# A hybrid attention layer's adaLN columns: wide products folded by VectorE, or one-column products

## The chip, the cores and the metric

The kernel runs on one core of one Trainium2 chip. The time is the device's time of one execution in microseconds (us); lower is better. A core has TensorE (PE, matrix products, with a weight load ahead of each product, PEld), VectorE (DVE), ScalarE (ACT), GpSimd (POOL) and SyncE (SP, which here only issues DMA transfers). Each engine works through its own queue in order; semaphores tie the queues together.

## The reference

One decoder layer over x of 2048 rows and 1024 columns, float32. Only the beginning matters here:

```python
mod = jax.nn.silu(c) @ w_ada[l] + b_ada[l]
shift, scale, gate = jnp.split(mod, 3, axis=-1)
h = rms_norm(x, g_pre[l]) * (1.0 + scale[:, None, :]) + shift[:, None, :]
proj = h @ w_in[l]
qa, ka, va, fa, za, qb, kb, vb, zb = jnp.split(proj, split_points, axis=-1)
...
y = jnp.concatenate([oa, ob], axis=-1) @ w_out[l]
x = x + gate[:, None, :] * rms_norm(y, g_post[l])
```

c is one row of 1024 numbers and w_ada has 1024 rows and 3 x 1024 columns, so shift and scale are two products of one row with a 1024 x 1024 matrix each. Between the projection and the output lie a causal attention with forget gates (8 heads) and a sliding-window attention with sinks (8 heads); the change doesn't touch them.

## The kernel before

The kernel is one long program. It begins with a block in which it makes the scale and the shift, normalises and turns the first 512 rows of x, and prepares the weights of the first two projections (named kb and vb). Behind the block a list of projection units runs over four chunks of 512 rows (chunk number ci); the next chunk is turned between the units of the present one. Then come window attention, the causal attention and the output projection. The order on each engine around the change is that of the statements, by hand.

**Tiles.** P is 128, KT is 8: the 1024 columns are 8 groups of 128, and k counts them. The projections need x turned: columns on partitions, rows along the tile. `hT[ci]` holds the turned chunk in two float16 parts, a high one and a low one (the rest), so that three float16 products stand for one of more precision.

**Scale and shift** (`half` 1 is the scale, 0 the shift). `load_ada` (L440) brings a part of w_ada, 128 rows by 1024 columns, 512 KB, into one of eight slots `wa`; sixteen parts are loaded, the scale's first. `sil` holds silu(c) as 8 columns; `silb` (L467) is each of these columns repeated 128 times. Each part goes one of two ways. `ada_pe` (L478) multiplies on TensorE with `silb` as weight and the part's columns moving, two products of 512 columns, into two banks of PSUM; so every partition holds the same row of 1024 results. `ada_dve` (L481) multiplies and adds on VectorE into `acc`; `ada_sum` (L488) adds this to the banks by a product with ones. `ada_col` (L491) turns the row into columns: VectorE multiplies each bank with the identity and sums over 128, two instructions a bank, four a half, so that entry (p, k) is result 128 k + p.

**Order of the scale's and shift's work.** On TensorE: six parts of the scale, its sum (L567), a small transpose for the weights' maxima (L572), the shift's parts 0, 3 and 5, later its part 7 and its sum (L603, L604). VectorE has the scale's parts 2 and 5 and the shift's 1, 2, 4 and 6. Four tiles of x (128 rows each, `load_x`) come between the shift's loads 2 and 3, four more behind the last. ScalarE squares each tile of x and sums by row (`squares`, L374); `root` makes the reciprocal root on VectorE, in small instructions; `normal(0)` multiplies the first four tiles by it on ScalarE.

**From the shift to the first turned column.** With the scale come `gcol`, which is g (1 + scale), and its absolute value `absg` (L596, L598); with the shift `shf` (L612) and its absolute value. `bnd` = 32 |gcol| + |shf| bounds what turned x can hold; its maximum over the 8 columns (L618), a transpose (L620), a maximum (L622) and a product with ones (L623) bring the largest one to every partition, and a power of two below it (`pow2_floor`, `pH`) scales `Gp` and `Shp` (L627, L628), which ScalarE's passes use as scale and bias.

**Turned x.** `turn(ci, k)` transposes four blocks on TensorE into one of five PSUM banks of the pool `ps_x` and gives back two steps: `scaled` writes `hf` (float32) and, for even k, the high part, each by a pass of ScalarE (L403); `split` copies the high part on VectorE for odd k (L407) and subtracts it for the low part (L408). In the block five turns stand ahead of the bound's work, then ScalarE squares the second chunk's four tiles (`squares(1)`, L608), and a loop over k (L632) runs the steps, the second chunk's root in parts from k = 2, and the last three turns. Outside the block `turn_x` does the same for the later chunks.

Of the kernel before, what the change touches and what calls it, by code (L numbers as in the profile page):

```python
# [10 lines left out]
F32 = mybir.dt.float32  # L11
# [4 lines left out]
ALU = mybir.AluOpType  # L16
AX = mybir.AxisListType

P = 128
S = 2048  # L20
D = 1024
KT = D // P
NB = S // P
CH = 512
# [17 lines left out]
def hybrid_layer(  # L42
# [17 lines left out]
    V, A, G, PE, SP = nc.vector, nc.scalar, nc.gpsimd, nc.tensor, nc.sync  # L60
# [10 lines left out]
    ps_x = psx.enter_context(tc.tile_pool(name="ps_x", bufs=5, space=PSUM, reuse_waits="tile"))  # L71
# [9 lines left out]
    def sm(n, tag):  # L81
        return small.tile([P, n], F32, tag=tag, name=tag)

    def pow2_floor(dst, src, bits_tag):

        t = sm(1, bits_tag)
        V.tensor_scalar(t[:], src, 1.0e-30, None, op0=ALU.max)
        V.tensor_scalar(dst.bitcast(I32), t[:].bitcast(I32), 0x7F800000, None, op0=ALU.bitwise_and)

    def rsqrt_mean(dst, ss, n):  # L90

        for _ in rsqrt_parts(dst, ss, n):
            pass
# [52 lines left out]
    ident = const.tile([P, P], F32, name="ident")  # L146
# [8 lines left out]
    ones = const.tile([P, P], F32, name="ones")  # L155
    sil = const.tile([P, KT], F32, name="sil")
# [17 lines left out]
    bk = [ps_bk.tile([P, CH], F32, name=f"bk{n}") for n in range(3)]  # L174
# [80 lines left out]
    def w_low(key, part, parts=2):  # L255
        raw, pw, sw, whl = wq[key]
        ks = slice(KT * part // parts, KT * (part + 1) // parts)
        V.scalar_tensor_tensor(whl[:, 1, ks], raw[:, ks], sw[:], whl[:, 0, ks], op0=ALU.mult, op1=ALU.subtract)
        if part == parts - 1:
            wq[key] = whl  # L260
            pws[key] = pw
# [112 lines left out]
    def squares(ci, us=range(4)):  # L374
        if ci not in rstd:
            rstd[ci] = sm(4, "ss"), sm(4, "rst")
        for u in us:
            junk = hst.tile([P, D], BF16, tag="junk", name="junk", bufs=1)
            A.activation(junk[:], xt[ci * 4 + u], AF.Square, accum_out=rstd[ci][0][:, u:u + 1])

    def root(ci):
        ss, rst = rstd[ci]
        rsqrt_mean(rst, ss[:], 4)

    def normal(ci, us=range(4)):
        for u in us:
            t, r = ci * 4 + u, rstd[ci][1][:, u:u + 1]
            if ci == 0:
                A.activation(xt[t], xt[t], AF.Copy, scale=r)
            else:  # L390
                V.tensor_scalar(xt[t], xt[t], r, None, op0=ALU.mult)

    def turn(ci, k):

        px = ps_x.tile([P, CH], F32, tag="x", name="px")
        for u in range(4):
            PE.transpose(px[:, u * P:(u + 1) * P], xt[ci * 4 + u][:, k * P:(k + 1) * P], ident[:])
        hf = hst.tile([P, CH], F32, tag="hf", name="hf")
        hi, lo = hT[ci][:, 0, k, :], hT[ci][:, 1, k, :]

        def scaled():
            for dst in ([hi] if k % 2 == 0 else []) + [hf[:]]:
                A.activation(dst, px[:], AF.Identity, scale=Gp[:, k:k + 1], bias=Shp[:, k:k + 1])  # L403

        def split():
            if k % 2:
                V.tensor_copy(hi, hf[:])  # L407
            V.tensor_tensor(lo, hf[:], hi, op=ALU.subtract)  # L408

        return scaled, split  # L410

    def turn_x(ci, k):
        scaled, split = turn(ci, k)
        after(1, scaled)
        after(2, split)
# [9 lines left out]
    start = ExitStack()  # L425
    st = start.enter_context(tc.tile_pool(name="start", bufs=1, reuse_waits="tile"))
    wad = start.enter_context(tc.tile_pool(name="wad", bufs=8, reuse_waits="tile"))
    with tc.manual_schedule():
# [9 lines left out]
        wa = {}  # L438
# [19 lines left out]
        cols = st.tile([P, 40], F32, name="cols")  # L458
# [4 lines left out]
        V.tensor_scalar(hc[:], cols[:, 0:8], 0.5, None, op0=ALU.mult)  # L463
        V.scalar_tensor_tensor(sil[:], th[:], 1.0, hc[:], op0=ALU.add, op1=ALU.mult)

        silb = st.tile([P, KT, P], F32, name="silb")
        V.tensor_copy(silb[:], sil[:].unsqueeze(2).broadcast_to([P, KT, P]))  # L467

        pm = {1: [ps_x.tile([P, CH], F32, tag="x", name="pm") for _ in range(2)], 0: [bk[1], bk[2]]}
        acc = [st.tile([P, D], F32, name=f"acc{n}") for n in range(2)]

        def ada_mm(half, lhsT, rows_, begin, end):
            for n in range(2):
                PE.matmul(pm[half][n][:], lhsT, rows_[:, n * CH:(n + 1) * CH], start=begin, stop=end)

        def ada_pe(half, k, begin=False, end=False):  # L478
            ada_mm(half, silb[:, k, :], wa[half, k], begin, end)

        def ada_dve(half, k, first_):  # L481
            if first_:
                V.tensor_scalar(acc[half][:], wa[half, k][:], sil[:, k:k + 1], None, op0=ALU.mult)
            else:
                V.scalar_tensor_tensor(acc[half][:], wa[half, k][:], sil[:, k:k + 1], acc[half][:],
                                       op0=ALU.mult, op1=ALU.add)

        def ada_sum(half, end):  # L488
            ada_mm(half, ones[:], acc[half], False, end)

        def ada_col(half, dst):  # L491

            for n in range(2):
                dg = acc[half][:, n * CH:(n + 1) * CH].rearrange("p (k n) -> p k n", k=4)
                V.tensor_tensor(dg, pm[half][n][:].rearrange("p (k n) -> p k n", k=4),
                                ident[:].unsqueeze(1).broadcast_to([P, 4, P]), op=ALU.mult)
                V.tensor_reduce(dst[:, 4 * n:4 * n + 4], dg, axis=AX.X, op=ALU.add)


        zero = st.tile([P, 2 * P], F32, name="zero")  # L500
# [49 lines left out]
        def col8(name):  # L550
            return st.tile([P, KT], F32, name=name)


        for k in (0, 1, 3, 4, 6, 7):
            ada_pe(1, k, k == 0)
# [8 lines left out]
        for t in range(4, 8):  # L564
            load_x(t)
        w_load("zb0", pieces("zb0"), SP)
        ada_sum(1, True)  # L567

        mx3 = st.tile([P, 2], F32, name="mx3")
        for n, key in enumerate(first[:2]):  # L570
            V.tensor_reduce(mx3[:, n:n + 1], wq[key][0][:], axis=AX.XY, op=ALU.max, apply_absolute_value=True)
        PE.transpose(bk[0][0:2, 0:P], mx3[:], ident[:])  # L572
        ada_pe(0, 0, True)
        ada_dve(0, 1, True)
        ada_dve(0, 2, False)
# [3 lines left out]
        V.tensor_scalar(dg3[:], ident[0:2, 0:2], m3[:], None, op0=ALU.mult)  # L579
        PE.matmul(bk[0][:, P:P + 2], ones[0:2, :], dg3[:], start=True, stop=True)  # L580
        ada_pe(0, 3)
        ada_pe(0, 5)
        squares(0)
        scl0 = col8("scl0")
        ada_col(1, scl0)
        V.tensor_copy(mxs[:, 0:2], bk[0][:, P:P + 2])
        for n, key in enumerate(first[:2]):
            wq[key].append(mxs[:, n:n + 1])
# [2 lines left out]
        w_high("kb")  # L591
        w_high("vb")
        scl1 = col8("scl1")
        V.tensor_tensor(scl1[:], scl0[:], cols[:, 24:32], op=ALU.add)
        gcol = col8("gcol")
        V.scalar_tensor_tensor(gcol[:], scl1[:], 1.0, cols[:, 8:16], op0=ALU.add, op1=ALU.mult)  # L596
        absg = col8("absg")
        V.scalar_tensor_tensor(absg[:], gcol[:], -1.0, gcol[:], op0=ALU.mult, op1=ALU.max)  # L598
        root(0)
        normal(0)  # L600
        ada_dve(0, 4, False)
        ada_dve(0, 6, False)
        ada_pe(0, KT - 1)  # L603
        ada_sum(0, True)  # L604
        w_low("kb", 0, 1)
        w_low("vb", 0, 1)
        turned = [turn(0, k) for k in range(5)]
        squares(1)  # L608
        shf0 = col8("shf0")
        ada_col(0, shf0)  # L610
        shf = col8("shf")
        V.tensor_tensor(shf[:], shf0[:], cols[:, 16:24], op=ALU.add)  # L612
        abss = col8("abss")
        V.scalar_tensor_tensor(abss[:], shf[:], -1.0, shf[:], op0=ALU.mult, op1=ALU.max)
        bnd = col8("bnd")
        V.scalar_tensor_tensor(bnd[:], absg[:], 32.0, abss[:], op0=ALU.mult, op1=ALU.add)
        bmx = st.tile([P, 1], F32, name="bmx")
        V.tensor_reduce(bmx[:], bnd[:], axis=AX.X, op=ALU.max)  # L618

        PE.transpose(bk[0][0:1, 0:P], bmx[:], ident[:])  # L620
        bm = st.tile([1, 1], F32, name="bm")
        V.tensor_reduce(bm[:], bk[0][0:1, 0:P], axis=AX.X, op=ALU.max)  # L622
        PE.matmul(bk[0][:, P:P + 1], ones[0:1, :], bm[:], start=True, stop=True)  # L623
        pow2_floor(pH[:], bk[0][:, P:P + 1], "p2t")
        ipH = st.tile([P, 1], F32, name="ipH")
        V.reciprocal(ipH[:], pH[:])
# [5 lines left out]
        for k in range(KT):  # L632
            turned[k][0]()
            turned[k][1]()
            if k >= 2:
                next(root1, None)
            if k + 5 < KT:
                turned.append(turn(0, k + 5))
# [865 lines left out]
    with tc.manual_schedule():  # L1504
# [25 lines left out]
        for s, stp_ in enumerate(steps):  # L1530
# [20 lines left out]
            half = (len(todo) + 1) // 2  # L1551
# [85 lines left out]
```

## Time and profile before

| | us |
|---|---|
| median of 3 runs | 1205.63 |
| lowest, highest | 1203.94, 1209.42 |
| the profiled execution | 1204.7 |
| its span, first to last instruction | 1202.7 |

| share of the span | busy us | instructions |
|---|---|---|
| TensorE products | 1150.1 (96%) | 10829 |
| TensorE weight loads | 692.2 (58%) | 10829 |
| VectorE | 918.0 (76%) | 2293 |
| ScalarE | 662.3 (55%) | 1100 |
| GpSimd | 114.8 (10%) | 231 |

The profile is one execution. Rows of instructions name the line of the kernel, the engine, the operation, the tile written and the tiles read, partitions by elements, and a count; in the order of time the first number is the start and the second the length of the whole group, and the bracket says how long the engine had been idle and who ended that. A float32 product of the kernel is recorded as two instructions. The length of a product is modelled and longer than its distance to the next. The granted clock is the share of TensorE's full clock that the hardware let through; it is half or full. In the rows of slices each digit is tenths of busy time in a fortieth of the span, 30 us.

### The profile page before, as it was taken

What the parts mean: (1) busy time and instruction counts of PE and PEld (TensorE: products, weight loads), DVE (VectorE), ACT (ScalarE), POOL (GpSimd) and SP (SyncE); (2) the same over time, 40 slices, a digit from 0 to 9 for tenths busy, and PEclk for the clock granted to TensorE, in tenths of its full rate; (3) what the DMA queues carried; (4) which work ended last, traced back from release to release, by engine and by line L of the source; (5) the groups of instructions that cost most, each with busy time, mean ns of one, the idle gap of its engine ahead of it and who ended that gap; (6) DMA issues with size and microseconds to landing.
All of it is one profiled execution on the core that took longest, in us unless ns stands there. A gap on an engine that the chain in (4) does not pass through costs nothing.

```text
span 1202.7 us, 27228 instructions
## 1 busy us (share of the span) xinstructions
PE 1150.1 (96%) x10829; PEld 692.2 (58%) x10829; DVE 918.0 (76%) x2293; ACT 662.3 (55%) x1100; POOL 114.8 (10%) x231
## 2 busy tenths in 40 slices
PE   5899899999999999999999999999999999999997
PEld 2466456765568976555555555555555565555553
DVE  7877577777877649688887899888688887767665
ACT  2784346465555512566766666676566788333231
POOL 2001012212222211010010110001000000000000
PEclk9899999999999999999999999999899999999999
DMA  9734333323233332433333332113311245455652
GB/s 332 269 106 101 94 86 91 59 78 91 84 93 69 49 75 50 65 85 67 76 61 78 86 61 74 39 45 76 36 42 42 79 132 176 145 169 182 203 167 85
DMA packets 87579, 120.22 MB, mean 100 GB/s; under 512 B 27508, under 2 KB 63388, under 8 KB 87452
## 3 DMA queue, kind: packets, MB, share of 16 engines
q1 hardware_dynamic: 76184, 85.69, 24.4%
q0 software_dynamic: 10832, 32.50, 12.5%
q8 instruction: 85, 1.39, 0.6%
q10 hardware_dynamic: 436, 0.28, 0.2%
q14 instruction: 42, 0.34, 0.1%
HBM read 71.04 MB, written 25.18 MB: 80 GB/s over the span
## 4 chain that ended last, share of the span: by engine, by line
PE 77%; DVE 8%; DMA 7%; issue 6%; ACT 2%; POOL 0%; SPq 0%; DVEq 0%; ACTq 0%; POOLq 0%
PE bk L314 28%; PE bk L1442 13%; PE bk L332 7%; PE sta L1290 4%; PE sta L1289 4%; PE bk L1240 4%; PE poa L1315 3%; PE poa L1313 3%; PE poa L1316 3%; DMA T<-rw 2%; PE pxb L885 2%; DMA wa<-in_w_ada_dram 2%; PE pss L852 2%; PE pob L904 2%; DVE a_m L1243 1%
## 5 line engine op out<-in xcount | busy, mean ns | idle before, releaser
L1296 ACT ACTIVATE p<-sta,lift,scl_qk 128x1024 f32<-128x1024 f32 (+2 forms) x160 | 171.9, 1074 | 151.7 <-PE sta L1290 88.3
L314 PE MATMUL bk<-hT,wh_qk 128*128 128x512 f16 x768 | 195.0, 378 | 0.0
L1442 PE MATMUL bk<-wohl,oz 128*128 128x512 f16 x768 | 172.2, 379 | 0.7 <-DVE oz L1429 0.7
L1243 DVE TENSOR_REDUCE a_m<-bk 128x1 f32<-128x512 f32 x192 | 130.5, 686 | 53.5 <-PE bk L1240 53.2
L1303 DVE TENSOR_TENSOR pha<-p,pha 128x1024 f16<-128x1024 f32 (+2 forms) x160 | 169.0, 1056 | 0.2 <-ACT pha L1300 0.2
L1300 ACT ACTIVATE pha<-p 128x1024 f16<-128x1024 f32 (+2 forms) x160 | 147.9, 924 | 5.8 <-PE poa L1316 1.3
L1442 PEld LDWEIGHTS <-oz 128*128 128x128 f16 x768 | 74.3, 99 | 82.2 <-DVE oz L1429 1.2
L1240 PE MATMUL bk<-T 66*128 66x512 f16 (+2 forms) x320 | 110.4, 349 | 10.5 <-DMA T<-rw 7.4
L1316 PE MATMUL poa<-vt,pha 128*128 128x65 f16 x1088 | 117.1, 193 | 1.1 <-DVE pha L1303 1.0
L1313 PE MATMUL poa<-vt,pha 128*128 128x65 f16 x1088 | 117.4, 194 | 0.3 <-DVE ona L1322 0.3
L1315 PE MATMUL poa<-vt,pha 128*128 128x64 f16 x1088 | 117.4, 195 | 0.0
L314 PEld LDWEIGHTS <-wh_qk 128*128 128x128 f16 x768 | 72.3, 97 | 74.4 <-issue 1.1
L1289 PE MATMUL sta<-T 128*128 128x512 f16 (+1 forms) x320 | 111.9, 350 | 1.3 <-ACT p L1296 1.3
L1313 PEld LDWEIGHTS <-pha 128*128 128x128 f16 x1088 | 102.1, 97 | 15.4 <-DVE ona L1322 1.8
L1290 PE MATMUL sta<-T 69*128 69x512 f16 (+1 forms) x320 | 110.8, 351 | 0.0
L1315 PEld LDWEIGHTS <-pha 128*128 128x128 f16 x1088 | 101.5, 97 | 11.3
L1316 PEld LDWEIGHTS <-pha 128*128 128x128 f16 x1088 | 101.4, 99 | 1.3 <-DVE pha L1303 1.3
L314 PE MATMUL bk<-hT,wh_za 128*128 128x512 f16 x384 | 101.4, 382 | 0.0
L332 PE MATMUL bk<-wh_va,hT 128*128 128x128 f16 x1536 | 90.9, 219 | 1.4 <-issue 1.4
L332 PEld LDWEIGHTS <-hT 128*128 128x128 f16 x1536 | 87.6, 98 | 6.3 <-issue 3.7
L314 PE MATMUL bk<-hT,wh_qb 128*128 128x512 f16 x384 | 87.4, 379 | 2.5 <-DVE qc L715 2.5
L314 PE MATMUL bk<-hT,wh_zb 128*128 128x512 f16 x384 | 89.2, 379 | 0.0
(492 smaller groups left out, 1852.3 us busy)
## 6 DMA issues: line engine op xcount, KB each, us to landing
hT<-in_x_dram SPq DMA_DIRECT2D x20, 512.0 KB
wa<-in_w_ada_dram SPq DMA_DIRECT2D x16, 512.0 KB
z_d<-tz POOLq DMA_DIRECT2D x32, 256.0 KB, 3.0
T<-stq SPq DMA_DIRECT2D x64, 128.0 KB
T<-o_d SPq DMA_DIRECT2D x16, 512.0 KB
T<-z_d SPq DMA_DIRECT2D x16, 512.0 KB
out_dram<-hT SPq DMA_DIRECT2D x15, 512.0 KB
xt<-in_x_dram SPq DMA_DIRECT2D x12, 512.0 KB
```

The source lines that it names most:

```text
L314: PE.matmul(ps, whl[:, a, k, :], hT[ci][:, b, k, :], start=(k == 0 and n == 0), stop=(k == KT - 1 and n == 2))
L332: PE.matmul(ps[:, u * P:(u + 1) * P], hT[ci][:, a, k, u * P:(u + 1) * P], whl[:, b, k, :], start=(k == 0 and n == 0), stop=(k == KT - 1 an ...
L1240: PE.matmul(mx[:, :w], T[0:XM, 0, i * P:(i + 1) * P], T[0:XM, 2, pc * CH:pc * CH + w], start=True, stop=True)
L1289: PE.matmul(self.st[:, o:o + w], T[:, 3, kb_], T[:, 1, qc], start=True, stop=False)
L1290: PE.matmul(self.st[:, o:o + w], T[0:XR, 2, kb_], T[0:XR, 0, qc], start=False, stop=not diag)
L1296: A.activation(self.p32[:, :self.w], self.st[:, :self.w], AF.Exp, scale=scl[f"qk{self.hd}"][:], bias=lift[:])
L1300: A.activation(self.ph[:, 0, :self.w], self.p32[:, :self.w], AF.Copy)
L1303: V.tensor_tensor(self.ph[:, 1, :self.w], self.p32[:, :self.w], self.ph[:, 0, :self.w], op=ALU.subtract)
L1313: PE.matmul(po[:, u, :], ph[:, 0, pq], vt[:, b, hd, 0:65], start=(self.first and n == 0 and u == 0), stop=False)
L1315: PE.matmul(po[:, u, 0:64], ph[:, 0, pq], vt[:, b, hd, 65:VW], start=False, stop=False)
L1316: PE.matmul(po[:, u, :], ph[:, 1, pq], vt[:, b, hd, 0:65], start=False, stop=(self.last and n == len(self.blocks) - 1))
L1442: PE.matmul(py, self.hl[:, i, k, :], w_slot(8 * j + k)[:, cc], start=(k == 0 and m_ == 0), stop=(k == KT - 1 and m_ == 2))
```

## The change

Scale and shift come out as columns at once: the part of w_ada becomes the weight, in 8 blocks of 128 columns, and the column `sil[:, k]` moves, one column a product. A half lies in 8 columns of one bank of the pool `bk`, no longer in two banks; `silb`, `ada_col` and its eight VectorE instructions go, and the banks' sums are read where they lie. `ada_sum` has `acc` as weight and one column of ones moving.

The bound is taken as 32 max |gcol| + max |shf| over each partition's columns: the scale's maximum `gmx` is made with the scale, and two products with the identity add both in one row of PSUM, in place of the transpose. This bound can be larger than the one before, since the two maxima may lie in different columns.

The order changes: two turns stand ahead of the bound's work in place of five, the third between the maximum's two products, the next two behind; three tiles of the second chunk are squared ahead of the loop and the fourth in it, behind k = 1; the root's parts begin at k = 3. In the first chunk ScalarE makes the high part for k = 0, 3 and 6, in place of 0, 2, 4 and 6; the later chunks stay as they were.

```diff
+        on_act = k % 2 == 0 if ci else k % 3 == 0
 
         def scaled():
-            for dst in ([hi] if k % 2 == 0 else []) + [hf[:]]:
+            for dst in ([hi] if on_act else []) + [hf[:]]:
                 A.activation(dst, px[:], AF.Identity, scale=Gp[:, k:k + 1], bias=Shp[:, k:k + 1])
 
         def split():
-            if k % 2:
+            if not on_act:
                 V.tensor_copy(hi, hf[:])
             V.tensor_tensor(lo, hf[:], hi, op=ALU.subtract)
...
-        silb = st.tile([P, KT, P], F32, name="silb")
-        V.tensor_copy(silb[:], sil[:].unsqueeze(2).broadcast_to([P, KT, P]))
-        pm = {1: [ps_x.tile([P, CH], F32, tag="x", name="pm") for _ in range(2)], 0: [bk[1], bk[2]]}
+        pm = {1: bk[2], 0: bk[1]}
...
-        def ada_mm(half, lhsT, rows_, begin, end):
-            for n in range(2):
-                PE.matmul(pm[half][n][:], lhsT, rows_[:, n * CH:(n + 1) * CH], start=begin, stop=end)
+        def ada_mm(half, rows_, rhs, begin, end):
+            for j in range(KT):
+                PE.matmul(pm[half][:, j:j + 1], rows_[:, j * P:(j + 1) * P], rhs, start=begin and j == 0, stop=end and j == KT - 1)
 
         def ada_pe(half, k, begin=False, end=False):
-            ada_mm(half, silb[:, k, :], wa[half, k], begin, end)
+            ada_mm(half, wa[half, k], sil[:, k:k + 1], begin, end)
...
         def ada_sum(half, end):
-            ada_mm(half, ones[:], acc[half], False, end)
-
-        def ada_col(half, dst):
-
-            for n in range(2):
-                dg = acc[half][:, n * CH:(n + 1) * CH].rearrange("p (k n) -> p k n", k=4)
-                V.tensor_tensor(dg, pm[half][n][:].rearrange("p (k n) -> p k n", k=4),
-                                ident[:].unsqueeze(1).broadcast_to([P, 4, P]), op=ALU.mult)
-                V.tensor_reduce(dst[:, 4 * n:4 * n + 4], dg, axis=AX.X, op=ALU.add)
+            ada_mm(half, acc[half], ones[:, 0:1], False, end)
...
         squares(0)
-        scl0 = col8("scl0")
-        ada_col(1, scl0)
...
-        V.tensor_tensor(scl1[:], scl0[:], cols[:, 24:32], op=ALU.add)
+        V.tensor_tensor(scl1[:], pm[1][:, 0:KT], cols[:, 24:32], op=ALU.add)
...
+        gmx = st.tile([P, 1], F32, name="gmx")
+        V.tensor_reduce(gmx[:], absg[:], axis=AX.X, op=ALU.max)
+        V.tensor_scalar(gmx[:], gmx[:], 32.0, None, op0=ALU.mult)
         root(0)
         normal(0)
         ada_dve(0, 4, False)
         ada_dve(0, 6, False)
+        PE.matmul(bk[0][0:1, 0:P], gmx[:], ident[:], start=True, stop=False)
         ada_pe(0, KT - 1)
         ada_sum(0, True)
         w_low("kb", 0, 1)
         w_low("vb", 0, 1)
-        turned = [turn(0, k) for k in range(5)]
-        squares(1)
-        shf0 = col8("shf0")
-        ada_col(0, shf0)
+        turned = [turn(0, k) for k in range(2)]
+        squares(1, (0, 1, 2))
         shf = col8("shf")
-        V.tensor_tensor(shf[:], shf0[:], cols[:, 16:24], op=ALU.add)
-        abss = col8("abss")
-        V.scalar_tensor_tensor(abss[:], shf[:], -1.0, shf[:], op0=ALU.mult, op1=ALU.max)
-        bnd = col8("bnd")
-        V.scalar_tensor_tensor(bnd[:], absg[:], 32.0, abss[:], op0=ALU.mult, op1=ALU.add)
+        V.tensor_tensor(shf[:], pm[0][:, 0:KT], cols[:, 16:24], op=ALU.add)
         bmx = st.tile([P, 1], F32, name="bmx")
-        V.tensor_reduce(bmx[:], bnd[:], axis=AX.X, op=ALU.max)
-
-        PE.transpose(bk[0][0:1, 0:P], bmx[:], ident[:])
+        V.tensor_reduce(bmx[:], shf[:], axis=AX.X, op=ALU.max, apply_absolute_value=True)
+
+        PE.matmul(bk[0][0:1, 0:P], bmx[:], ident[:], start=False, stop=True)
         bm = st.tile([1, 1], F32, name="bm")
         V.tensor_reduce(bm[:], bk[0][0:1, 0:P], axis=AX.X, op=ALU.max)
+        turned.append(turn(0, 2))
         PE.matmul(bk[0][:, P:P + 1], ones[0:1, :], bm[:], start=True, stop=True)
+        turned += [turn(0, k) for k in (3, 4)]
         pow2_floor(pH[:], bk[0][:, P:P + 1], "p2t")
...
         for k in range(KT):
             turned[k][0]()
             turned[k][1]()
-            if k >= 2:
+            if k == 1:
+                squares(1, (3,))
+            if k >= 3:
                 next(root1, None)
```

## The prediction

> **What bounds the kernel now.** I read the page first, then the chain that ended last, then the engines in order of time up to 56 us. The page:
>
> ```profile
> span 1202.7 us, 27228 instructions
> ...
> PE   5899899999999999999999999999999999999997
> ...
> DMA  9734333323233332433333332113311245455652
> ```
>
> TensorE is busy nearly everywhere but in the first slice of 30 us, where transfers take nine tenths. The change touches only the beginning, up to 56 us; the 1145 us behind it all need its output, so what it gains or loses there is handed on. The chain there (start, us, what):
>
> ```profile
> 25.71 10.87 DMA wa<-in_w_ada_dram
> ...
> 36.62 2.86 PE bk L476 x6
> ...
> 39.50 0.70 DVE acc L495
> ...
> 42.87 0.17 DVE bmx L618
> ...
> 43.09 0.28 PE bk L620
> ...
> 43.40 0.29 DVE bm L622
> ...
> 43.73 0.39 PE bk L623 x2
> ...
> 45.18 0.78 ACT hT L403
> ```
>
> The shift's last weights land at 36.58. Then come 2.86 us of products, VectorE instructions from 39.50 to 43.04, the turned maxima, and at 45.18 ScalarE's first pass over the turned x.
>
> **The change, part by part.** *The products.* A part was two float32 products of 512 columns, recorded as four instructions. It becomes eight of one column, sixteen pairs of weight load and product. The rows, first by line (PEld is the weight load; behind the count stand the shortest, middle and longest in ns), then in order of time (start, length of the group):
>
> ```profile
> L397 PEld LDWEIGHTS px<-ident,xt x96: 138/141/230, 39.7 to 112.7; 128*128 128x128 f32 x96
> L1514 PEld LDWEIGHTS bk<-w_mx,ones x2: 189/190/192, 438.5 to 438.6; 128*128 128x128 f32 x2
> ```
>
> ```profile
> 9.69 1.19 PE L476 MATMUL pm<-wa,silb 128*128 128x512 f32 x1 [4.50 <-DMA wa<-in_w_ada_dram]
> ...
> 36.62 1.98 PE L476 MATMUL bk<-wa,silb 128*128 128x512 f32 x4 [0.23 <-DMA wa<-in_w_ada_dram]
> 38.45 1.88 PE L476 MATMUL bk<-acc,ones 128*128 128x512 f32 x4
> ...
> 40.16 2.10 PEld L397 LDWEIGHTS px<-ident,xt 128*128 128x128 f32 x19 [0.29 <-issue]
> ...
> 50.15 0.66 PEld L397 LDWEIGHTS px<-ident,xt 128*128 128x128 f32 x3 [0.20 <-issue]
> ...
> 438.54 0.30 PEld L1514 LDWEIGHTS bk<-w_mx,ones 128*128 128x128 f32 x2
> 438.59 0.33 PE L1514 MATMUL bk<-w_mx,ones 128*128 128x1 f32 x2
> ...
> 438.96 0.16 DVE L118 TENSOR_SCALAR sc_h<-bk 128x1 int32<-128x1 int32 x1 [0.51 <-PE bk L1514]
> ```
>
> Old: (38.45 - 36.62)/4 = 0.46 us an instruction with the first one's start, 1.8 a part. New: two loads of 0.19 in 0.30 stand 0.11 apart, and the turned x's loads (2.10 - 0.14)/18 = 0.109; sixteen make 1.74. So TensorE gains and loses next to nothing at the same clock. No row shows a long run of one-column products, so the bounds are wide: 0.08 a pair (the two products of L1514 together last 0.33, one of them about 0.25) to 0.215 ((0.66 - 0.23)/2, the turned x's loads at 50.15, at half the clock). I take 0.109, the row of the same load. Parts before the last wait for their transfers as now.
>
> *The columns.* For the scale, VectorE loses four instructions of about 0.69. They end in nothing: behind them the root waits for ScalarE's fourth square:
>
> ```profile
> 30.53 0.19 ACT L379 ACTIVATION_READ_ACCUMULATOR junk<-xt 128x1 f32 x1
> 30.75 0.17 DVE L97 TENSOR_SCALAR rs_v<-ss 128x4 f32<-128x4 f32 x1
> ```
>
> VectorE comes there 2.7 us sooner and waits; the two new instructions for the scale's maxima (0.2 each) fit in that. Without that cover they would cost 0.4. For the shift the four instructions (39.50 to 42.25) were on the chain. New chain, from 36.62: 32 pairs of 0.109 bring the last to 40.11; it ends 0.25 later, and L118 began 0.04 after such an end, so the shift starts at 40.40. It takes 0.20; its maximum, with the way to TensorE (42.87 to 43.09), 0.22: ready at 40.82. TensorE meanwhile turns two columns of x, eight times 0.109 from 40.22, until 41.09; so the maxima's product starts at 41.09 and not at 40.82, which costs 0.27. It is in two instructions now, 0.11 more than the 0.31 from L620 to L622: 41.51. From L622 to L623 0.33, from L623 to ScalarE's pass 1.45: **43.29** instead of 45.18, so 1.9 us gained. Behind the waiting maxima's product stand the third column's turns (0.44 from 41.31, done before 41.84), behind L623's those of two more; nobody needs these before k = 2 and later.
>
> *At no cost:* the product of the scale's maxima stands ahead of the shift's last part, where TensorE waits for the transfer until 36.62; without that wait it would be 0.2. The dropped wide copy of silu(c) ended before the first part had landed (the product at 9.69 waits for it), so nothing is gained.
>
> *The loop behind it.* Here the gain is mostly eaten. In the loop's window, and at its end:
>
> ```profile
> L403 ACT ACTIVATE hf<-px,Shp,Gp 128x512 f32<-128x512 f32 x8 | 5.9, 803 | 0.0
> L408 DVE TENSOR_TENSOR hT<-hf,hT 128x512 f16<-128x512 f32 x8 | 5.5, 690 | 1.8 <-ACT hf L403 1.7
> L403 ACT ACTIVATE hT<-px,Shp,Gp 128x512 f16<-128x512 f32 x4 | 3.2, 796 | 2.2 <-DVE pfl L630 2.2
> ...
> L407 DVE CAST hT<-hf 128x512 f16<-128x512 f32 x4 | 1.7, 422 | 0.0
> ```
>
> ```profile
> 41.84 1.06 ACT L379 ACTIVATE junk<-hT 128x1024 bf16<-128x1024 f32 x1 [0.17 <-DMA hT<-in_x_dram]
> ...
> 46.66 0.69 DVE L408 TENSOR_TENSOR hT<-hf,hT 128x512 f16<-128x512 f32 x1 [1.52 <-ACT hf L403]
> ...
> 53.49 0.15 DVE L109 TENSOR_TENSOR rs_t<-rs_y 128x4 f32<-128x4 f32 x1
> ...
> 53.95 0.68 DVE L408 TENSOR_TENSOR hT<-hf,hT 128x512 f16<-128x512 f32 x1
> 54.55 0.42 DVE L407 CAST hT<-hf 128x512 f16<-128x512 f32 x1
> 55.01 0.69 DVE L408 TENSOR_TENSOR hT<-hf,hT 128x512 f16<-128x512 f32 x1
> ```
>
> ScalarE's twelve passes follow about 0.66 apart, until 53.3. VectorE waited 1.7 in all near the start and is the late one at the end (55.01). The change takes one pass from ScalarE but puts the fourth square (1.06 and 0.19 for reading the sum, about 1.2 together) behind k = 1, and gives VectorE a fifth copy. VectorE's steps by these rows: copy to subtraction 0.46, subtraction to the next 0.61, a root step of three 0.46, so the root's first four 0.6; and a pass can be read 0.82 after its start (46.66, two passes after 45.18). New: the first subtraction comes 1.48 after 43.29, at 44.77, and k = 1 is done at 46.5. k = 2 waits for a pass that starts at 43.29 + 3 x 0.66 + 1.2 = 46.47 and is read at 47.3: done 48.35. k = 3 has passes at 47.13 and 47.79 and is subtracted at 48.6. From there VectorE never waits: 0.61 + 0.6, k = 4 1.07, step 0.46, k = 5 1.07, step 0.46, k = 6 0.61, step 0.46, copy 0.46 bring the last subtraction to **54.4** instead of 55.0. So **0.6 us** are left of 1.9. The square had cover before (it ended at 43.0, ahead of 45.18); in the loop it has none.
>
> *Behind the loop* TensorE (22.27 of 24 us) and VectorE (21.83) leave little slack in the next 24 us, so the 0.6 us go on:
>
> ```profile
> 56.00:80.00 24.00, 22.27 (x197) 15.62 (x196) 21.83 (x58) 18.72 (x31) 0.00 (x0) 1.00 0.54 174
> ```
>
> The x loads on SP's queue wait for the last turned column, and would start 1 to 2 us sooner; nothing is late by them. No transfer is added or changes its place in a queue; slots of the scale's weights come free at the same pace.
>
> *Sum.* The profiled execution took 1204.7 us (span 1202.7, and 2.0 around it). 1204.7 - 0.6 = **1204.1**. The median of the three runs shown is 0.9 above that execution, their spread 1203.9 to 1209.4.
>
> **Rivals.** *The clock gate stays at half (slower).* The granted clock (the column after the five engines) in windows of 3.41 us:
>
> ```profile
> 10.93:14.34 3.41, 3.41 (x5) 1.27 (x5) 3.24 (x7) 0.00 (x0) 0.00 (x0) 1.00 1.02 340
> 24.58:28.00 3.42, 2.26 (x8) 0.94 (x6) 3.35 (x6) 2.15 (x4) 0.00 (x0) 1.00 1.02 407
> 48.48:51.89 3.41, 3.41 (x12) 1.77 (x11) 3.05 (x12) 3.41 (x7) 0.00 (x0) 0.50 0.17 23
> 847.19:850.61 3.42, 2.77 (x33) 2.40 (x34) 1.20 (x4) 0.91 (x2) 0.08 (x1) 0.50 0.48 63
> 956.42:959.83 3.41, 1.47 (x28) 0.86 (x26) 3.31 (x8) 3.41 (x4) 0.00 (x0) 1.00 0.53 154
> 959.83:963.25 3.42, 3.08 (x30) 2.19 (x31) 3.24 (x6) 1.29 (x4) 0.00 (x0) 0.50 0.17 40
> ```
>
> The kernel starts at half, whatever the column says before the first change on record: the first product of L476 took 1.19, four later ones 1.88 together. Windows with TensorE busy 3.08 and 3.41 are followed by the full clock, 2.77 is not; from full, 1.47 is followed by half, 2.26 is not. What counts as busy these rows can't say: all their work streams 64 to 512 columns. A one-column product streams next to nothing in its 0.109. If loads don't count, the gate never opens during the products: 112 pairs for the scale and 80 for the shift at 0.215 are 41.3 us from 9.66, so 51.0, against 40.1; from transfers the bound moves to TensorE. With the small products between them (0.5) and turns at half pace (0.9 + 0.4 + 0.3 more until L623) ScalarE's first pass comes near 56, 10.7 us later than before, and the loop is 1.3 us longer (1.9 - 0.6): 12.0 in all, **1216.7**. It decides from about 0.13 a pair: there the 32 pairs behind the last transfer cost 32 x 0.019 = 0.6, the gain. For it: the start is at half, and nothing but the products could open the gate. Against: a recorded one-column product lasts 0.25 (0.33 for two), so by the records TensorE would be busy without a gap.
>
> The Trainium skill, page "TensorE: Matmul & The Clock Gate", section "Part 4: PE-mode transpose", says that turns don't count as busy the same way as products and don't open the gate. The trace disagrees: in 48.48 to 51.89 0.85 us were turns, and without them its 2.56 would be less than the 2.77 that opened nothing. By the rule, work that computes little would leave this gate shut as well, and the time would be this rival's 1216.7; as the trace stands, it lends that no more weight.
>
> *The loop does not eat it.* If VectorE's steps are hidden and the 1.9 us pass whole, 1202.8. Against it: its steps from 48.6 on leave no gap. *Partly open:* the gate opens in the middle of the products; between, 1206 to 1213. *The change doesn't do what it says:* products pace at transfers and no column step was late; then the start stays and the loop's 1.3 us are lost, 1206.0. Against it: 39.50 to 42.25 lies on the chain with no other wait.
>
> **How the numbers follow.** Chances: forecast 0.40, whole gain 0.08, no gain 0.06, partly open 0.11 (half of it over 0.5%), gate shut 0.32, faster by something unseen 0.03. About 0.5% (6 us) is what a measurement of this kernel tells from no change. Faster 0.03; same 0.40 + 0.08 + 0.06 + 0.05 = 0.59; slower 0.32 + 0.06 = 0.38. The forecast's own range is 1201 to 1208, by the runs' spread; as the shut gate holds a third, the range reaches to its 1216.7 with 1.3 above: 1201 to 1218.
>
> **What would show it.** Right: one-column pairs 0.11 apart, the granted clock full before 20 us, shift's addition near 40.4, ScalarE's first pass near 43.3, last subtraction of the loop near 54.4, with VectorE without gaps before it. Wrong: pairs at 0.2, products that last beyond 45 us, x turned after 50; or VectorE with gaps at the loop's end. The square behind k = 1 should show as a gap of about 0.7 on VectorE ahead of k = 2's copy.

## The result and the profile after

| | before | after |
|---|---|---|
| median, us | 1206.94 (4 runs) | 1220.03 (4 runs) |
| lowest to highest | 1203.94 to 1209.42 | 1217.52 to 1224.28 |
| the profiled execution | 1204.7 | 1217.52 |

The changed kernel is slower: 1.0113 times the time before, with an interval from 1.0075 to 1.0151. That is outside the range of 1201 to 1218, and it is the rival "the clock gate stays at half" that happened (the gate is what switches the granted clock between half and full). Its working had given 1216.7 for the profiled execution, which took 1217.52.

The page of the changed kernel: the span, and TensorE's and the transfers' busy share in slices of 30 us.

```profile
span 1215.8 us, 27511 instructions
...
PE   7989899999999999999998999999999999999997
...
DMA  9453243323323322423424421212411336446652
```

Before, the first two digits of TensorE were 58 and those of the transfers 97. Now TensorE has 79 and the transfers 94: the engine that waited for data has become the one that data waits for. The chain of work says the same (start, us, what):

```profile
2.23 6.99 DMA wa<-in_w_ada_dram
...
9.36 24.02 PE bk L474 x112
...
33.61 3.21 PE bk L474 x16
...
37.33 6.92 PE bk L474 x32
...
44.76 6.92 PE bk L474 x32
51.68 1.81 PE px L397 x8
53.49 0.51 PE bk L607 x2
54.00 1.05 PE px L397 x4
55.05 0.51 PE bk L611 x2
55.56 1.06 PE px L397 x4
...
56.64 0.10 ACT hT L404
```

Before, the chain ran through a transfer until 36.58. Here no transfer is on it after 9.22; from 9.36 to ScalarE's first pass at 56.64 it is TensorE without a gap (the pieces left out there are its own small products, 1.3 us together, and 0.02 of issue), and 41 us of it are the 192 products of L474. Only the last piece is doubtful: beside the turns from 55.56 on run VectorE's small instructions behind L611 (55.60 to 56.60), and in the run with 128 columns below it is these that the same pass waits for. The order of time, with the start, the length of the group and, in the bracket, the idle time before it:

```profile
9.36 20.61 PE L474 MATMUL bk<-sil,wa 128*128 128x1 f32 x96 [4.69 <-DMA wa<-in_w_ada_dram]
...
48.13 3.55 PE L474 MATMUL bk<-ones,acc 128*128 128x1 f32 x16
51.54 1.95 PE L397 MATMUL px<-ident,xt 128*128 128x128 f32 x8
...
58.14 1.97 PE L397 MATMUL px<-ident,xt 128*128 128x128 f32 x8
```

```profile
51.72 0.17 DVE L603 TENSOR_TENSOR shf<-bk,cols 128x8 f32<-128x8 f32 x1 [4.71 <-PE bk L474]
...
58.12 0.69 DVE L409 TENSOR_TENSOR hT<-hf,hT 128x512 f16<-128x512 f32 x1 [1.52 <-ACT hf L404]
...
60.49 0.43 DVE L408 CAST hT<-hf 128x512 f16<-128x512 f32 x1 [0.55 <-ACT hf L404]
...
67.56 0.69 DVE L409 TENSOR_TENSOR hT<-hf,hT 128x512 f16<-128x512 f32 x1
```

A one-column product is recorded with 0.35 us, so the distance of two is (20.61 - 0.35)/95 = 0.213, and it is the same at the last sixteen: (3.55 - 0.35)/15 = 0.213. The turned x's loads stand as far apart, and eight of its products still take 1.97 at 58.14. So the whole stretch ran at half the clock. (The profile's clock column shows 1.00 there; it knows only changes, and none is on record before 60 us.) From first product to first turn 51.54 - 9.36 = 42.2 us go by; the prediction had the first turn at 40.22.

The sum of the difference: ScalarE's first pass is at 56.64 instead of 45.18, 11.5 later. From there to the loop's last subtraction it is 67.56 - 56.64 = 10.92 instead of 55.01 - 45.18 = 9.83, another 1.1. These 12.6 of the span's 13.1 us are lost before 70 us and never made up.

### The profile page after: what moved, and what is told of

Its sections match the earlier page's. It is cut to its first block, busy times and chain, and to the rows that moved or that the text cites. A ratio compares the mean times of both kernels' runs of the same rounds, so it can differ in the third digit from the quotient of the medians.

```text
span 1215.8 us, 27511 instructions
## 1 busy us (share of the span) xinstructions
PE 1170.0 (96%) x10976; PEld 726.1 (60%) x10976; DVE 912.4 (75%) x2285; ACT 660.8 (54%) x1099; POOL 114.8 (9%) x231
## 4 chain that ended last, share of the span: by engine, by line
PE 78%; DVE 8%; issue 6%; DMA 5%; ACT 2%; POOL 1%; SPq 0%; DVEq 0%; ACTq 0%; POOLq 0%
PE bk L314 27%; PE bk L1433 13%; PE bk L332 7%; PE sta L1281 4%; PE sta L1280 4%; PE bk L1231 4%; PE bk L474 3%; DMA T<-rw 3%; PE poa L1306 3%; PE poa L1307 3%; PE poa L1304 3%; PE pxb L876 2%; PE pss L843 2%; PE pob L895 2%; PE bk L1396 1%
```

## The experiments

At this point the theory was: the gate doesn't go by whether a product or a load is in hand, but by how many columns pass through TensorE; one-column products pass next to none, so they neither open the gate nor keep it open. Three rivals: first, a one-column product has a pace of 0.21 of its own, whatever the clock; second, any product in hand counts as soon as it moves more than a column or so; third, one-column products can't open the gate but keep it open once something has opened it. Beside this stood a smaller question: whether the column form gains anything once the gate is open, and whether the loop eats it.

### 128 equal columns in place of one

The rest of the change stays. Each product carries the column of silu(c) 128 times, and of 128 equal columns of results only the first is used. The results fill two banks a half, as before the change, so VectorE reads them with two additions a half in place of one (not in the cut shown).

```diff
-        pm = {1: bk[2], 0: bk[1]}
+        silb = st.tile([P, KT, P], F32, name="silb")
+        V.tensor_copy(silb[:], sil[:].unsqueeze(2).broadcast_to([P, KT, P]))
+        pm = {1: [ps_x.tile([P, CH], F32, tag="x", name="pm") for _ in range(2)], 0: [bk[1], bk[2]]}
...
-                PE.matmul(pm[half][:, j:j + 1], rows_[:, j * P:(j + 1) * P], rhs, start=begin and j == 0, stop=end and j == KT - 1)
+                PE.matmul(pm[half][j // 4][:, (j % 4) * P:(j % 4 + 1) * P], rows_[:, j * P:(j + 1) * P], rhs,
+                          start=begin and j % 4 == 0, stop=end and j % 4 == 3)
...
-            ada_mm(half, wa[half, k], sil[:, k:k + 1], begin, end)
+            ada_mm(half, wa[half, k], silb[:, k, :], begin, end)
...
-            ada_mm(half, acc[half], ones[:, 0:1], False, end)
+            ada_mm(half, acc[half], ones[:], False, end)
```

> Same as the changed kernel, but each product moves 128 equal columns in place of one (same 192 weight loads of 128 columns). Gate theory (one-column products do not count as busy, so the clock stays at half): the clock opens before 20 us as in the kernel before, loads stand 0.11 us apart, ScalarE's first pass near 43.5 us, time 1203 to 1207, ratio to before 0.997 to 1.003. Rival 1 (long runs of small float32 products with a weight load each take 0.21 us a pair at any clock): loads 0.21 apart with the clock open, ratio about 1.010. Rival 2 (the loss is the reordered loop and queue order, not the products): loads 0.11 apart and still 1.008 or more.

Measured: 1205.22 us (10 runs) beside 1205.92 for the kernel before (13 runs), a ratio of 0.9997 with an interval from 0.9981 to 1.0012. The order of time, and windows of the same profile (the last three columns are the granted clock, the share of the transfers and GB/s):

```profile
15.51 7.68 PE L477 MATMUL pm<-silb,wa 128*128 128x128 f32 x64 [0.27 <-DMA wa<-in_w_ada_dram]
...
31.75 6.53 PE L477 MATMUL bk<-silb,wa 128*128 128x128 f32 x32 [4.58 <-DMA wa<-in_w_ada_dram]
...
45.51 0.78 ACT L404 ACTIVATE hT<-px,Shp,Gp 128x512 f16<-128x512 f32 x1 [3.64 <-DVE pfl L628]
...
56.45 0.69 DVE L409 TENSOR_TENSOR hT<-hf,hT 128x512 f16<-128x512 f32 x1
```

```profile
27.18:30.59 3.41, 0.00 (x0) 0.00 (x0) 2.10 (x15) 2.95 (x7) 0.00 (x0) 1.00 1.02 408
30.59:34.00 3.41, 2.25 (x10) 2.25 (x11) 1.96 (x14) 3.20 (x4) 0.00 (x0) 0.50 1.03 410
34.00:37.42 3.42, 3.42 (x18) 3.42 (x17) 3.04 (x4) 3.34 (x4) 0.00 (x0) 0.50 1.02 408
37.42:40.80 3.38, 3.38 (x30) 3.04 (x29) 1.95 (x2) 3.20 (x6) 0.00 (x0) 1.00 1.05 376
```

The number of products and of weight loads is that of the changed kernel. Only the columns that move are more, 128 times as many, and the products take less time, not more: 7.68 us for 64 of them from 15.51 on, 0.12 apart. TensorE waits for transfers again. The loss of 13 us is gone, with the new order of the loop and of the turns still in place. An idle window (27.18 to 30.59, while TensorE waits for the shift's third part) shuts the gate, and two windows at half follow, until the second of them, busy throughout, opens it again; so the shift's products behind the wait run at half and ScalarE's first pass is at 45.51, no sooner than before, where 43.5 had been expected.

### 64 equal columns

As above with 64 columns, one bank for each half.

```diff
-                PE.matmul(pm[half][:, j:j + 1], rows_[:, j * P:(j + 1) * P], rhs, start=begin and j == 0, stop=end and j == KT - 1)
+                PE.matmul(pm[half][:, j * 64:(j + 1) * 64], rows_[:, j * P:(j + 1) * P], rhs, start=begin and j == 0, stop=end and j == KT - 1)
...
-            ada_mm(half, wa[half, k], sil[:, k:k + 1], begin, end)
+            ada_mm(half, wa[half, k], silb[:, k, 0:64], begin, end)
```

> As n128, but 64 equal columns move, which fill half of a pair's time at either clock (64 x 2 cycles of 256). If the gate counts streamed columns, half a window is too little to open it (0.81 of a window did not open it before): clock at half until the first projection, pairs 0.213 us apart, time 1216 to 1219 like the changed kernel. If it counts any product in flight, or weight loads, it opens before 20 us and the time is 1203 to 1207.

Measured: 1218.85 us in one run. In the order of time:

```profile
9.46 20.71 PE L477 MATMUL bk<-silb,wa 128*128 128x64 f32 x96 [4.88 <-DVE ang L514]
...
51.96 1.92 PE L397 MATMUL px<-ident,xt 128*128 128x128 f32 x8
```

20.71 us for 96, as with one column: the gate stayed shut, although a product moved 64 columns in each 0.213 us without a gap. Between 64 and 128 columns lies the point from which such a row opens it; where, wasn't tried. The weight loads alone don't open it, since they stood in the same gapless row here as in the changed kernel.

### Opening the gate ahead, by products and by turns

Twenty products of 128 float32 columns go ahead of the scale's and shift's (8 and 12, on both sides of the first transpose); nobody reads them. In the second kernel there are forty transposes of the same size instead (16 and 24).

```diff
+        for _ in range(8):
+            PE.matmul(bk[2][:, 0:P], ones[:], ones[:], start=True, stop=True)
         PE.transpose(bk[0][:, :P], rows[:], ident[:])
+        for _ in range(12):
+            PE.matmul(bk[2][:, 0:P], ones[:], ones[:], start=True, stop=True)
```

> The changed kernel with 20 products of 128 float32 columns ahead of the first part (results thrown away), from about 1.3 to 9.5 us, so that the gate should be open when the one-column products begin. Gate theory: first pairs 0.11 us apart, then back to 0.213 after one or two windows of 3.4 us; time 1211 to 1217. Rival 1 (pace independent of the clock): pairs 0.21 apart from the first on. Rival 3 (one-column products hold an open gate open but cannot open it): 0.11 apart until the first wait, time 1203 to 1208.

> As warm_prod, with 40 transposes of 128 columns in place of the 20 products ahead of the first part. If transposes count for the gate as products do, it opens near 7 us as there, the first one-column loads stand 0.11 us apart, and it shuts again one or two windows later. If they do not count, it never opens before the first projection and the first loads stand 0.213 apart.

Measured: 1222.01 us with the products, 1220.55 with the transposes, one run each. The kernel with the products, weight loads (PEld) and products in the order of time, then its windows:

```profile
9.65 1.86 PEld L478 LDWEIGHTS bk<-sil,wa 128*128 128x128 f32 x16 [1.09 <-DVE ang L512]
...
12.75 16.41 PE L478 MATMUL bk<-sil,wa 128*128 128x1 f32 x80 [1.15 <-DMA wa<-in_w_ada_dram]
...
55.84 0.78 ACT L404 ACTIVATE hT<-px,Shp,Gp 128x512 f16<-128x512 f32 x1 [6.89 <-DVE pfl L623]
```

```profile
10.26:13.68 3.42, 2.27 (x21) 2.18 (x21) 3.25 (x7) 0.00 (x0) 0.00 (x0) 1.00 1.02 321
13.68:17.09 3.41, 3.41 (x19) 3.41 (x18) 3.24 (x6) 0.00 (x0) 0.00 (x0) 0.50 1.03 412
```

The kernel with the transposes, which the profile records as MATMUL:

```profile
5.11 3.90 PE L462 MATMUL bk<-ident,ones 128*128 128x128 f32 x24
9.16 1.92 PE L478 MATMUL bk<-sil,wa 128*128 128x1 f32 x16 [0.15 <-DVE ang L512]
12.35 1.95 PE L478 MATMUL bk<-sil,wa 128*128 128x1 f32 x16 [1.27 <-DMA wa<-in_w_ada_dram]
15.02 13.81 PE L478 MATMUL bk<-sil,wa 128*128 128x1 f32 x64 [0.72 <-DMA wa<-in_w_ada_dram]
```

Here is the 0.109 of the prediction: sixteen one-column pairs take 1.86 of weight loads at 9.65, 0.11 apart, while the clock is full. So they have no pace of their own; they follow the clock. And they don't keep it: 10.26 to 13.68 holds nothing but such pairs, 2.27 us busy by the records, and behind it the clock is half. The window of the kernel before from 24.58, with 2.26 busy in wide products, was followed by the full clock. From 12.75 the products stand (16.41 - 0.35)/79 = 0.203 apart on the mean, and ScalarE's first pass is only 0.8 us sooner than in the changed kernel. Opening it ahead is no remedy. The time with the products lies above the 1211 to 1217 expected, and its one execution is 4.5 us longer than the profiled one of the changed kernel in spite of those 0.8, though within that kernel's scatter. The trace places this behind the loop. TensorE stands still for 1.96 us from 387.37, in the middle of a row of products, where the changed kernel has only 0.87 at a later row (a stop that comes back in the next experiment). And near 1000 us VectorE waits 5.23 us for a transfer (`T<-z_d`, until 1003.76) and two windows at half follow, 1006.96 to 1013.79, neither of which the changed kernel's execution has. Why isn't shown.

### The scale wide, the shift in columns

The scale's products are those of before (with `ada_col` for it); the shift's and all the rest are those of the change. The kernel was run twice.

```diff
         def ada_mm(half, rows_, rhs, begin, end):
+            if half:
+                for n in range(2):
+                    PE.matmul(pm[half][n][:], rhs, rows_[:, n * CH:(n + 1) * CH], start=begin, stop=end)
+                return
...
-            ada_mm(half, wa[half, k], sil[:, k:k + 1], begin, end)
+            ada_mm(half, wa[half, k], silb[:, k, :] if half else sil[:, k:k + 1], begin, end)
```

> The changed kernel with the scale made as before (products of 512 columns, folded by VectorE) and only the shift by one-column products. Gate theory: the clock opens near 14 us; the idle window before 31 us shuts it as in the kernel before, and the shift's one-column products leave it shut: last pairs 0.213 apart, ScalarE's first pass near 50 us, time 1209 to 1212. Rival 1 gives the same pace and is not told apart here; rival 2 gives about 1217 whatever the pace.

> The same kernel as scale_wide, timed, because its one execution ended 14.3 us after the kernel before although its loop ended 5.7 us later. If the other 9 us are half-clock windows that fall by chance in later stages, the median over rounds is 1.004 to 1.006 times the kernel before (1210.5 to 1213). If they belong to the kernel, it stays near 1.011.

Measured: 1218.66 in a single run; in the second set 1213.13 (4 runs), 1.0072 times the kernel before of the same set (1204.11), interval 1.0051 to 1.0092. In the order of time, and windows, of the first:

```profile
24.20 1.84 PE L481 MATMUL bk<-sil,wa 128*128 128x1 f32 x16
...
41.23 3.55 PE L481 MATMUL bk<-ones,acc 128*128 128x1 f32 x16
...
49.74 0.78 ACT L404 ACTIVATE hT<-px,Shp,Gp 128x512 f16<-128x512 f32 x1 [8.89 <-PE px L397]
```

```profile
26.13:29.54 3.41, 0.23 (x2) 0.14 (x2) 3.13 (x12) 2.96 (x7) 0.00 (x0) 1.00 1.02 406
29.54:32.96 3.42, 2.60 (x13) 2.60 (x13) 2.91 (x21) 2.86 (x4) 0.00 (x0) 0.50 1.03 406
...
50.02:53.43 3.41, 3.32 (x14) 2.13 (x13) 1.79 (x3) 3.41 (x6) 0.00 (x0) 0.50 0.00 0
```

The same line in one kernel: sixteen pairs in 1.84 at the full clock, in 3.55 at half. The scale's wide products open the gate; the wait for the shift's third part shuts it, as in the run with 128 columns, but the one-column products behind the wait don't open it again, and it is half until 53.43. ScalarE's first pass comes 4.6 us later than before instead of 11.5. The shift's columns alone thus cost 4.6 of the 11.5 us. The time is longer than that explains: with the loop's 1.1 they make 5.7 us, 0.47%, just below the interval of 0.51% to 0.92%. The rest, some 3 us at the middle of the interval, arises behind the loop. Expected had been 1.004 to 1.006 if it was chance and about 1.011 if it belonged to the kernel; 1.0072 is neither. The trace of the second set places 1.8 of it at a stop of TensorE in the middle of a row of products, which the kernel before goes through without one (108 products in 6.20 us from 370.83):

```profile
376.51 4.08 PE L332 MATMUL bk<-wh_va,hT 128*128 128x128 f16 x70
382.43 2.28 PE L332 MATMUL bk<-wh_va,hT 128*128 128x128 f16 x38 [1.84 <-issue]
```

"issue" means that TensorE waited for nothing that the profile shows. Each execution here has such a stop somewhere between 380 and 435 us; the kernel before has one of 1.42 us, ending at 408.12, and this one a second of 1.29, ending at 412.01. VectorE's instructions, matched one by one with those of the kernel before, run 5.7 us late at 350 and 7.5 late at 430. In the first execution the stop at this row is 2.18 us long and is followed by a window at half (384.52 to 387.94). What sets the length of these stops stays open. Most of what is left of the 3 us is windows at half that fall elsewhere than in the execution before (one from 648.87, for instance, where that has none).

### The column form with the gate open and the loop of before

Two kernels ask what the column form is worth when its products open the gate. The first has 128 columns and the old loop: high parts on ScalarE for even k, all four squares ahead, the root from k = 2. The second has, besides, four products of 512 columns, thrown away, where TensorE waits for the shift's third part.

```diff
-        on_act = k % 2 == 0 if ci else k % 3 == 0
+        on_act = k % 2 == 0
...
-        squares(1, (0, 1, 2))
+        squares(1)
...
-            if k == 1:
-                squares(1, (3,))
-            if k >= 3:
+            if k >= 2:
```

```diff
         PE.matmul(bk[0][:, P:P + 2], ones[0:2, :], dg3[:], start=True, stop=True)
+        keep = ps_x.tile([P, CH], F32, tag="x", name="keep")
+        for n in range(4):
+            PE.matmul(keep[:], ones[:], silb[:, 0:4, :].rearrange("p k n -> p (k n)"), start=True, stop=True)
```

> n128 with the loop's order of the kernel before (all four squares ahead of the loop, ScalarE's high parts at k = 0, 2, 4, 6, root parts from k = 2). Theory: the reordered loop costs about 1.1 us of its own (first pass to eighth subtraction 9.8 us before, 10.9 to 11.0 in the changed kernel and n128), so this loop takes 9.8 to 10.0 us again, and the time lies 1 us under n128, ratio to before 0.997 to 1.000. Rival: VectorE's fifth copy and the square cost nothing, the loop keeps 10.9 because late turns hold it; then no difference from n128.

> n128_oldloop with four wide products (128 by 512 columns, results thrown away) where TensorE waits for the shift's third part, to keep the clock open there. Theory: no half-clock window between 20 and 40 us, all the shift's loads 0.11 us apart, ScalarE's first pass near 43.5 us, the loop's end near 53.4, ratio 0.996 to 0.999, 1 to 2 us under n128_oldloop. Rival: the transfers set the shift's end and the clock does not matter there; then equal to n128_oldloop.

Measured: 1203.7 us (12 runs) for the first and 1204.0 (12 runs) for the second, beside 1204.11 for the kernel before (23 runs): ratios of 0.9993 (0.9982 to 1.0005) and 1.0002 (0.9986 to 1.0018). Neither can be told from no change; for the second, 0.996 to 0.999 and a time 1 to 2 us under the first had been expected, and that was missed. In the order of time, the first kernel:

```profile
44.84 0.78 ACT L404 ACTIVATE hT<-px,Shp,Gp 128x512 f16<-128x512 f32 x1 [2.07 <-DVE pfl L628]
...
54.67 0.69 DVE L409 TENSOR_TENSOR hT<-hf,hT 128x512 f16<-128x512 f32 x1
```

and the second, with a window of it:

```profile
27.36 3.70 PE L582 MATMUL keep<-silb,ones 128*128 128x512 f32 x8
...
36.76 2.05 PE L477 MATMUL bk<-silb,wa 128*128 128x128 f32 x16 [0.20 <-DMA wa<-in_w_ada_dram]
...
43.76 0.78 ACT L404 ACTIVATE hT<-px,Shp,Gp 128x512 f16<-128x512 f32 x1 [0.58 <-DVE pfl L631]
...
53.59 0.69 DVE L409 TENSOR_TENSOR hT<-hf,hT 128x512 f16<-128x512 f32 x1
...
147.44 0.28 PE L853 MATMUL pss<-kst,stb 64*128 64x128 f16 x4 [2.79 <-ACT stb L730]
```

```profile
29.10:32.50 3.40, 2.81 (x12) 1.43 (x11) 1.52 (x11) 3.25 (x6) 0.00 (x0) 1.00 1.03 407
```

With the old loop it is 54.67 - 44.84 = 9.83 us from the first pass to the last subtraction, to the hundredth that of the kernel before; with the changed loop it was 56.45 - 45.51 = 10.94 in the run with 128 columns. So the new order of passes, square and root costs 1.1 us with the clock full as with it half. With the gap filled the gate stays open, and ScalarE's first pass comes 45.18 - 43.76 = 1.4 us sooner than before, 7.0 us behind the start of the shift's last products (36.76), where the prediction had counted 6.7 (36.62 to 43.29). These 1.4 us are 0.12% of the time, less than the interval can show. In the profiled execution they don't reach the end: at 147.44 TensorE has waited 2.79 us for `stb`, which hangs on a transfer (`qs<-qf`), and it starts only 0.67 sooner than in the kernel before, where it waited 1.42. The window of that wait, 145.20 to 148.60, has TensorE busy for 0.72, and the next one is at half, which the kernel before has nowhere near; by 200 us the instructions stand 1.0 later than there.

## Why the prediction was wrong

**The products, the step that failed.** "I take 0.109, the row of the same load", and "So TensorE gains and loses next to nothing at the same clock": the 0.109 is the right distance at the full clock (1.86 for sixteen in the run with products ahead), and the clock was not the same. All 192 pairs stood 0.213 apart, the upper bound that the prediction had from the turned x at half the clock (0.215). What it decided between was not two prices of a load but whether the gate opens, and for that it gave the forecast 0.40 and the shut gate 0.32.

**The evidence that was weighed wrongly.** "By the records TensorE would be busy without a gap" stood against the rival. The records did show that (the chain has no gap from 9.36 on), and it was worth nothing: the length of a record is modelled, and the gate went by the columns. The argument on the other side stood in the same paragraph, that a one-column product streams next to nothing and that all rows of before stream 64 to 512 columns, and it was right. The runs with 64 and 128 columns show it: the same products and loads, and only the columns differ.

**The rival's own working** held: the first pass "near 56" was at 56.64, the loop's loss of 1.3 was 1.1, and 12.0 in all was 12.8 between the two profiled executions. The range still ended too low. Its 1218 was this rival's time with 1.3 added, and the rival's time was worked out from one execution, which lies 2.2 us below the median of the four runs before; the after runs lie from 1217.52 to 1224.28, and a scatter like that of before, over 5 us, should have been added on that side.

**Turns and the gate.** The prediction set the Trainium skill, page "TensorE: Matmul & The Clock Gate", section "Part 4: PE-mode transpose", against the trace: by it turns don't count as busy. The run with forty transposes disagrees with the rule as well: behind them one-column pairs stood 0.11 apart ((1.92 - 0.25)/15 from 9.16, and 1.95 for the next sixteen), so the gate was open, and nothing but transposes had run. By the rule those sixteen would have taken 3.55. The rule thus gave no support to the rival; that one-column products don't count is another matter, which no sentence of that section says.

**The columns.** The chain without VectorE's four instructions was right where the gate was open: 7.0 us instead of the 6.7 counted. In the changed kernel it is 56.64 - 51.72 = 4.92 from the shift's addition to the first pass where 2.9 had been counted, because the turns and small products on it ran at half the clock too. And an open gate wouldn't have been enough for 43.29: where nothing filled the wait for the shift's third part, that wait shut the gate for the next parts of the shift even with 128 columns, and the first pass came at 45.51 and 44.84; filled, at 43.76. The prediction had no term for that.

**The loop.** Right in size: VectorE waits 0.55 ahead of k = 2's copy at 60.49 ("a gap of about 0.7") and has no gap behind k = 3. The old loop in the same kernel gives the 1.1 back; which of the three moves in it (pass, square, root) costs how much wasn't separated. With the gap filled 1.4 less 1.1 would leave 0.3 where 0.6 had been forecast; no run has both, so this is worked out and not measured.

**The covers.** "Slots of the scale's weights come free at the same pace" and the root that waits for ScalarE's fourth square held only as long as TensorE waited for transfers. SyncE's queue before and after (the length is the time from the first of the five loads to the last):

```profile
20.59 5.45 SPq L442 DMA_DIRECT2D wa<-in_w_ada_dram  x5
```

```profile
23.17 8.10 SPq L443 DMA_DIRECT2D wa<-in_w_ada_dram  x5
```

The last of the shift's weights were asked for at 31.3 instead of 26.0. And VectorE stood idle for 8.26 us, until 33.65, for the weights' maxima, whose products were queued on TensorE behind the scale's; ScalarE waited for what follows from them.

None of this added to the 11.5 us, since TensorE had no gap of its own; it shows that the covers were borrowed from the engine that had been idle.

## What to carry to other kernels

Before exchanging which operand is the weight and which one moves, count the columns that move per weight load, above all at a kernel's start or behind a wait, where the clock is half: a row of loads with few columns (1 and 64 here, per load of 128) looks fully busy in the records and runs at half the clock for as long as it lasts. Where thin products must stand there, moving the column 128 times over cost nothing here and opened the gate. And if the likeliest cases of a forecast hang on one switch, the forecast is the question which way it goes, and the range needs the runs' scatter on both sides.

## What the runs showed that was not expected

- *64 columns don't open the gate, 128 do,* with the same loads and no gap in either. One-column pairs shut an open gate behind the first window that held little else (10.26 to 13.68).
- *A single wait can cost two windows.* In the run with 128 columns 3.41 us without products were followed by 6.8 us at half, though TensorE was busy for 2.25 of the first 3.41 of these. Filling the gap with thrown-away products kept the gate open there, and made no difference to the whole time that could be told.
- *TensorE can stop in the middle of a row of products without a wait in the profile:* once or twice in each execution here between 380 and 435 us, for 0.47 to 2.18 us at a time, longest in the kernels with products or turns ahead and with the wide scale. Why isn't shown.
- *The windows are 3.41 us long and their edges lie elsewhere in each execution*: the gate opened at 14.34 before and at 13.5 with 128 columns, and shut at 13.68 with products ahead. The Trainium skill, the same page, section "Part 1: The HAM clock gate (the "warmup" mystery)", calls the window 3413 ns and free-running; these edges agree. So the same kernel meets its waits with other windows each time: the 13 runs of the kernel before in the first set spread from 1202.41 (mean granted clock 0.992) to 1210.45 (0.986), though another run at 0.986 took 1205.99. That this is the whole of the scatter isn't shown.
